# A long convolution's frequency loop on one NeuronCore: four PSUM banks written in one run of matmuls, a sum moved into the inverse transform, and row scales for two row blocks at once

## The chip, the cores and the metric

The kernel runs on one core of a Trainium2 chip. The metric is device microseconds of one execution; lower is better. Two times are compared only where they differ by more than the runs of one kernel do.

## The reference

One layer works on x of 2048 positions by 1024 channels, in float32. Two thirds of the projected channels go through a gated convolution over the whole length, done in the frequency domain, and the rest through a pooling branch:

```python
h = rms_norm(x, pre_g)
p = h @ w_in
hy = short_conv(p[..., :HYENA_IN])            # v and two gates, 512 channels each
k_f = two_sided_spectrum(hyena_filters(...))  # two filters of 2L samples for each channel
y = v
for o in range(2):
    y = gates[o] * (irfft(rfft(y, 2 * L) * k_f[:, o], 2 * L)[:, :L] + y * d)
y_h = rms_norm(y * silu(z_h), norm_h_g)
y_p = rms_norm(multiscale_pool(u_p) * silu(z_p), norm_p_g)
out = concat(y_h, y_p) @ w_out
return x + rms_norm(out, post_g)
```

## The kernel before

TensorE is written PE, VectorE DVE, ScalarE ACT, GpSimd POOL, SyncE SP. P is 128. The program has four parts, one after the other in the profile: projections, filters and pooling (to 646 us), eight frequency loops (646 to 1241), a short rest of the last gate (to 1258), and the output stage (1258 to 1404).

**The transforms.** The 512 channels are taken as four groups q of 128, and the convolutions as o = 0 and 1. Each transform has a stage of 128x128 matmuls (`s1`, `s1k`, and `gate` or `py1` on the way back), a transpose in blocks of 32 on DVE (`trans`), and a stage of 32x32 matmuls, which is the frequency loop `gloop(o, q)`. `BS[q]` holds the signal's half-done transform, `BK[o, q]` that of the filter. `gx`, `gk` and `gi` are tables of cosines and sines, laid out for 32x32 matmuls.

**The loop.** `gloop` returns a list of pieces for eight values of m. `PB` is one PSUM tile of four banks, [128, 4 banks, 4 slots, 128]: a matmul of row group i writes 32 partitions of one slot of one bank, and each piece touches all four banks. The pieces are:

- `kern(m)`: 32 matmuls transform the filter into slots 2 and 3 (L735, table `gk`), and ACT copies both slots to the SBUF tile `kk` (L742).
- `mult(m)`: 32 matmuls transform the signal into slots 0 and 1 (L735, table `gx`), DVE multiplies both slots by `kk` into `yt` (L748), and POOL adds the two halves of `yt` (L749).
- `back(m)`: 16 matmuls take the sum back into slot 2 (L756, table `gi`), and ACT copies it into `BS` (L757).

The list is `kern(0)`, `mult(0)` behind `kern(1)`, and then `back(m-1)`, `kern(m+1)`, `mult(m)` in turn, with `back(7)` at the end. The trace records each float32 matmul twice, so that 32 matmuls show as x64.

**What stands between the pieces.** `run(main, *sides)` writes the program's order by hand: the main list's pieces stand at even distances, and the pieces of the side lists are dealt among them. The sides of a loop prepare and finish other channel groups: `pre_k` and `pre_s` or `post0` (matmuls L603 to L605 in groups of six into PSUM tile `s` or `py`), and `fills`, the pooling half of the output product (L834 to L836, twelve 512-column matmuls into `fp`). The eight loops are called so, with fewer sides in the last:

```python
run(gloop(0, 0), seq(pre_k(0, 1), pre_s(1)), fills(5, 9))
...
run(gloop(1, 3, held), post1(2), [lambda ct=ct: split_wo(...) for ct in range(4)])
```

A scheduler may then move instructions a little; each engine runs its own list in order, and an instruction that waits holds back all that stand behind it on that engine.

**The output stage.** For each of 16 row blocks l2, `out_mm` writes two halves dh of 512 channels, 12 matmuls each (`mm_out`, L834 to L836), into two banks of `PB`. `finish` then has DVE scale both halves and add the pooling half `o` that a DMA brings (L965), ACT square and sum each half (L968), DVE add the two sums (L972) and make the reciprocal root `rp` in nine short operations (`rstd`, L189 to L200), DVE scale by `rp` and the gain (L979), POOL add x (L980), and SP send the rows out. `split_y`, `py1` and `stat_y` prepare the next four row blocks meanwhile.

## Time and profile before

| | |
|---|---|
| time, median of 3 runs | 1406.27 us (1402.15 to 1408.11) |
| the profiled execution's own time | 1406.32 us |
| its span in the trace | 1404.1 us |
| mean granted TensorE clock | 0.93 |
| PE busy | 1204.8 us (86% of the span) |
| DVE busy | 775.3 us (55%) |
| POOL busy | 484.6 us (35%) |
| ACT busy | 416.8 us (30%) |

The span runs from the first to the last instruction that the profiler recorded; the execution's own time is 2.2 us more. Shares of busy time are means over stages. A number in brackets behind a row of the timeline is the engine's idle time just before, with the instruction that ended it.

### The profile page before, as it was taken

Reading aid. Unit: us, or ns where it says so; the run is one execution under the profiler, and the core shown is the slowest. Engines: PE = TensorE matmul, PEld = TensorE weight load, DVE = VectorE, ACT = ScalarE, POOL = GpSimd, SP = SyncE. Lnnn points to the kernel's source line nnn. Section 1 sums busy time; section 2 is a strip of 40 time slices with the busy share of each in tenths; the row PEclk is TensorE's granted clock in tenths of the full one; section 3 lists DMA queues with packets and bytes.
Section 4 is the critical chain, followed back from the end, with each engine's and each line's share of the span. In section 5 each row is a group of like instructions: output and inputs, shape, how many; then the busy total and the mean of one; then the engine's idle time right before and its main releaser. Section 6 shows DMA issues by size and latency. Waiting matters only on the chain. (4 is left out here: it accounts for less than half of the span.)

```text
span 1404.1 us, 35240 instructions
## 1 busy us (share of the span) xinstructions
PE 1204.8 (86%) x15528; PEld 938.8 (67%) x15528; DVE 775.3 (55%) x1255; ACT 416.8 (30%) x643; POOL 484.6 (35%) x436
## 2 busy tenths in 40 slices
PE   7999999999999989979888887989788846477775
PEld 5788888788889989956556564657465534256554
DVE  6962664465467657635355645373655543137665
ACT  7521202121121121033435353343353532222211
POOL 2211104145518557532143432121343421223433
PEclk9999999999999999989999988999999976579999
DMA  7222304222333352287322324444313322053563
GB/s 247 74 79 75 95 26 124 81 97 93 132 104 95 114 147 91 75 289 237 122 89 61 105 70 133 137 120 137 96 62 110 119 78 85 2 168 129 182 210 128
DMA packets 102481, 162.15 MB, mean 115 GB/s; under 512 B 9257, under 2 KB 58169, under 8 KB 101049
## 3 DMA queue, kind: packets, MB, share of 16 engines
q1 hardware_dynamic: 100504, 156.94, 35.1%
q8 instruction: 121, 1.98, 0.6%
q10 hardware_dynamic: 1648, 2.44, 0.5%
q0 software_dynamic: 176, 0.53, 0.1%
q14 instruction: 32, 0.25, 0.1%
HBM read 113.22 MB, written 45.61 MB: 113 GB/s over the span
## 5 line engine op out<-in xcount | busy, mean ns | idle before, releaser
L749 POOL TENSOR_TENSOR yt<-yt 128x512 f32<-128x512 f32 x64 | 82.3, 1286 | 260.7 <-DVE yt L748 258.1
L557 PE MATMUL nm<-wh,XH 128*128 128x256 f32 x512 | 144.7, 283 | 8.0 <-DVE a L564 7.1
L748 DVE TENSOR_TENSOR yt<-PB,kk 128x1024 f32<-128x1024 f32 x64 | 78.0, 1219 | 121.3 <-PE PB L735 121.0
L559 PE MATMUL nm<-wh,XL 128*128 128x256 f32 x512 | 144.7, 283 | 0.0
L558 PE MATMUL nm<-wl,XH 128*128 128x256 f32 x512 | 144.7, 283 | 0.0
L564 DVE SCALAR_TENSOR_TENSOR a<-nm,r_nat,wc 128x256 f32<-128x256 f32 x192 | 81.5, 475 | 50.6 <-DMA wc<-cw 14.1
L557 PEld LDWEIGHTS nm<-wh,XH 128*128 128x128 f32 x512 | 97.7, 191 | 9.1 <-DVE a L564 8.3
L324 PE MATMUL mm<-XH,wh 128*128 128x512 f32 x256 | 103.0, 402 | 0.0
L756 PE MATMUL PB<-yt,gi 32*32 32x128 f32 x2048 | 35.3, 303 | 78.3 <-POOL yt L749 78.3
L326 PE MATMUL mm<-XH,wl 128*128 128x512 f32 x256 | 102.2, 399 | 0.0
L325 PE MATMUL mm<-XL,wh 128*128 128x512 f32 x256 | 101.5, 396 | 0.0
L559 PEld LDWEIGHTS nm<-wh,XL 128*128 128x128 f32 x512 | 96.7, 189 | 0.0
L558 PEld LDWEIGHTS nm<-wl,XH 128*128 128x128 f32 x512 | 96.6, 189 | 0.0
L735 PE MATMUL PB<-BS,gx 32*32 32x128 f32 x4096 | 77.5, 317 | 12.7 <-ACT kk L742 10.8
L630 DVE STREAM_TRANSPOSE BS<-BS 128x1024 f32<-128x1024 f32 x64 | 74.2, 1213 | 22.6 <-ACT BS L713 12.8
L735 PE MATMUL PB<-BK,gk 32*32 32x128 f32 x4096 | 75.7, 309 | 11.7 <-ACT BS L757 10.1
L756 PEld LDWEIGHTS PB<-yt,gi 32*32 32x32 f32 x2048 | 16.1, 108 | 102.1 <-POOL yt L749 101.6
L757 ACT COPY BS<-PB 128x512 f32<-128x512 f32 x64 | 39.8, 622 | 148.8 <-PE PB L756 148.8
L742 ACT COPY kk<-PB 128x1024 f32<-128x1024 f32 x64 | 64.8, 1012 | 59.5 <-PE PB L735 59.2
L735 PEld LDWEIGHTS PB<-BS,gx 32*32 32x32 f32 x4096 | 49.9, 112 | 43.9 <-ACT kk L742 18.4
L735 PEld LDWEIGHTS PB<-BK,gk 32*32 32x32 f32 x4096 | 48.8, 109 | 39.7 <-ACT BS L757 23.5
L686 POOL TENSOR_TENSOR sd<-ab 128x512 f32<-128x512 f32 x32 | 54.2, 1692 | 60.8 <-DVE ab L682 60.7
(216 smaller groups left out, 3030.8 us busy)
## 6 DMA issues: line engine op xcount, KB each, us to landing
fy<-yp_d SPq DMA_DIRECT2D x32, 512.0 KB
dec<-t_dec SPq DMA_DIRECT2D x30, 512.0 KB
wr<-w SPq DMA_DIRECT2D x16, 512.0 KB
ut<-v_d SPq DMA_DIRECT2D x32, 256.0 KB
op_d<-fo SPq DMA_DIRECT2D x32, 256.0 KB
gt<-g_d SPq DMA_DIRECT2D x32, 256.0 KB
o<-op_d SPq DMA_DIRECT2D x32, 256.0 KB
xt<-x SPq DMA_DIRECT2D x16, 512.0 KB
```

Of the source, the lines that this page charges most:

```text
L324: T.matmul(ps, wh, XH[lb][:, d], start=(d == 0), stop=False)
L325: T.matmul(ps, wh, XL[lb][:, d], start=False, stop=False)
L326: T.matmul(ps, wl, XH[lb][:, d], start=False, stop=(d == NT - 1))
L557: T.matmul(ps, xh[:, d, ls], wh, start=(d == 0), stop=False)
L558: T.matmul(ps, xh[:, d, ls], wl, start=False, stop=False)
L559: T.matmul(ps, xl[:, d, ls], wh, start=False, stop=(d == NT - 1))
L564: V.scalar_tensor_tensor(out=a[s], in0=ps, scalar=r_nat[:, l2:l2 + 1], in1=wc[:, s], op0=ALU.mult, op1=ALU.mult)
L630: V.transpose(out=ap, in_=ap)
L735: ins = T.matmul(PB[32 * i:32 * i + 32, j, slot + k], tab[js, 4 * m + i, k], B[js, 2 * m + i // 2, :, i % 2], start=True, stop=True)
L742: S.copy(out=kk, in_=PB[:, :, 2:4])
L748: V.tensor_tensor(out=yt, in0=PB[:, :, 0:2], in1=kks.pop(m), op=ALU.mult)
L749: G.tensor_tensor(out=yt[:, :, 0], in0=yt[:, :, 0], in1=yt[:, :, 1], op=ALU.add)
```

## The change

A loop step is now one function, `step(t)`, which writes all four slots in one run of up to 80 matmuls and then reads them. It is called for t = -1 to 8, so the list has 10 pieces where it had 24.

- The way back for t-1 takes both halves of the product `cd` and adds them in PSUM: 32 accumulating matmuls into slot 3, in place of the POOL addition and 16 matmuls. `gi` is twice as large.
- The signal's transform for t has 16 matmuls into slot 0, where 32 went into slots 0 and 1: the second half was the first with other signs, which the tables `gk` and `gi` now hold. `gx` is half as large.
- The filter's transform for t+1 keeps its 32 matmuls, into slots 1 and 2.
- The readers follow: DVE multiplies slot 0, broadcast over two halves, by `kk` (L753 of the kernel after); ACT copies slot 3 into `BS` (L756) and slots 1 and 2 into the next `kk` (L762).
- `PB` has a pool of its own, closed ahead of the output stage, which takes its two halves from a pool of four one-bank tiles `po`.
- `finish` is split. `scale` has one square over 1024 elements in place of two over 512; `norm` makes `rp` for two row blocks at once (twelve operations on two elements in place of ten on one, twice). The last two row blocks are done alone, and the buffers of `o` go by pairs.

```diff
     psB = pool(ph2, "psB", 1, PS)
 
-    PB = psB.tile([P, 4, 4, P], F32, name="PB")
+    pst = ExitStack()
+    psL = pool(pst, "psL", 1, PS)
+    PB = psL.tile([P, 4, 4, P], F32, name="PB")
...
     def gloop(o, q, after=None):
         u = f"{o}{q}"
-        kks, yts = {}, {}
+        kks, cds = {}, {}
         order = [(j, (j + d) % 4) for d in range(4) for j in range(4)]
-        def fwd(B, tab, m, slot):
-            for k in range(2):
-                for j, i in order:
-                    js = slice(32 * j, 32 * j + 32)
-                    ins = T.matmul(PB[32 * i:32 * i + 32, j, slot + k], tab[js, 4 * m + i, k],
-                                   B[js, 2 * m + i // 2, :, i % 2], start=True, stop=True)
-            return ins
-
-        def kern(m):
-            fwd(BK[o, q], gk, m, 2)
-            kk = wp.tile([P, 4, 2, P], F32, tag="kk", name=f"kk{u}_{m}", bufs=2)
-            S.copy(out=kk, in_=PB[:, :, 2:4])
-            kks[m] = kk
-
-        def mult(m):
-            fwd(BS[q], gx, m, 0)
-            yt = fp.tile([P, 4, 2, P], F32, tag="yt", name=f"yt{u}_{m}", bufs=3)
-            V.tensor_tensor(out=yt, in0=PB[:, :, 0:2], in1=kks.pop(m), op=ALU.mult)
-            G.tensor_tensor(out=yt[:, :, 0], in0=yt[:, :, 0], in1=yt[:, :, 1], op=ALU.add)
-            yts[m] = yt
-
-        def back(m):
-            yt = yts.pop(m)
-            for i, j in order:
-                js = slice(32 * i, 32 * i + 32)
-                ins = T.matmul(PB[32 * j:32 * j + 32, i, 2], gi[js, m, j], yt[js, j, 0], start=True, stop=True)
-            S.copy(out=BS[q][:, 2 * m:2 * m + 2].rearrange("p a c i -> p a i c"),
-                   in_=PB[:, :, 2].rearrange("p (a i) c -> p a i c", i=2))
-            if after:
-                after(m, ins)
-
-        r = [lambda: kern(0)]
-        for m in range(8):
-            if m:
-                r.append(lambda m=m: back(m - 1))
-            if m + 1 < 8:
-                r.append(lambda m=m: kern(m + 1))
-            r.append(lambda m=m: mult(m))
-        r.append(lambda: back(7))
-        return r
+        def step(t):
+            if t > 0:
+                cd = cds.pop(t - 1)
+                for k in range(2):
+                    for i, j in order:
+                        js = slice(32 * i, 32 * i + 32)
+                        ins = T.matmul(PB[32 * j:32 * j + 32, i, 3], gi[js, k, t - 1, j], cd[js, j, k],
+                                       start=(k == 0), stop=(k == 1))
+            for m, B, tab, slots in ((t, BS[q], gx, (0,)), (t + 1, BK[o, q], gk, (1, 2))):
+                if 0 <= m < 8:
+                    for k, sl in enumerate(slots):
+                        for j, i in order:
+                            js = slice(32 * j, 32 * j + 32)
+                            w = tab[js, 4 * m + i, k] if len(slots) > 1 else tab[js, 4 * m + i]
+                            T.matmul(PB[32 * i:32 * i + 32, j, sl], w, B[js, 2 * m + i // 2, :, i % 2],
+                                     start=True, stop=True)
+            if 0 <= t < 8:
+                cd = fp.tile([P, 4, 2, P], F32, tag="cd", name=f"cd{u}_{t}", bufs=3)
+                V.tensor_tensor(out=cd, in0=PB[:, :, 0:1].broadcast_to([P, 4, 2, P]), in1=kks.pop(t), op=ALU.mult)
+                cds[t] = cd
+            if t > 0:
+                S.copy(out=BS[q][:, 2 * t - 2:2 * t].rearrange("p a c i -> p a i c"),
+                       in_=PB[:, :, 3].rearrange("p (a i) c -> p a i c", i=2))
+                if after:
+                    after(t - 1, ins)
+            if t < 7:
+                kk = wp.tile([P, 4, 2, P], F32, tag="kk", name=f"kk{u}_{t + 1}", bufs=2)
+                S.copy(out=kk, in_=PB[:, :, 1:3])
+                kks[t + 1] = kk
+        return [lambda t=t: step(t) for t in range(-1, 9)]
...
+    pst.close()
+    psO = pool(pst, "psO", 1, PS)
...
-                ps = PB[:, 2 * (i % 2) + dh].rearrange("p s c -> p (s c)")
+                ps = psO.tile([P, 512], F32, tag="po", name=f"po{l2}_{dh}", bufs=4)
...
-    def finish(lb, rr, i, pss):
+    hs = (slice(0, 512), slice(512, 1024))
+    live = {}
+    def scale(lb, rr, i, pss):
         l2 = 4 * lb + i
         xt = wp.tile([P, D], F32, tag="kk", name=f"xt{l2}", bufs=2)
         Q.dma_start(out=xt, in_=xv[:, l2])
-        if l2 % 5 > 2:
-            o_ = abp.tile([P, D], F32, tag="ab", name=f"o{l2}", bufs=2)
-        else:
-            o_ = wp.tile([P, D], F32, tag=("sd", "dd")[l2 % 2], name=f"o{l2}", bufs=2)
+        tg = ("sd", "dd", "ab")[l2 // 2 % 3]
+        o_ = (abp if tg == "ab" else wp).tile([P, D], F32, tag=tg, name=f"o{l2}", bufs=2)
         for dh in range(2):
             Q.dma_start(out=o_[:, dh * 512:dh * 512 + 512], in_=op_d[dh, l2])
-        hs = (slice(0, 512), slice(512, 1024))
+        if l2 % 2 == 0 or l2 == 15:
+            live["ss"] = op.tile([P, 2], F32, tag="ss2", name=f"ss{l2}", bufs=2)
+        ss = live["ss"][:, l2 % 2:l2 % 2 + 1]
         s2 = op.tile([P, 2], F32, tag="s2", name=f"s2{l2}", bufs=2)
         for dh, ds in enumerate(hs):
             V.scalar_tensor_tensor(out=o_[:, ds], in0=pss[dh], scalar=rr[:, i:i + 1], in1=o_[:, ds],
                                    op0=ALU.mult, op1=ALU.add)
-            sq = fp.tile([P, 512], F32, tag="sq", name=f"sq{l2}_{dh}", bufs=2)
-            S.activation(out=sq, in_=o_[:, ds], func=AF.Square, accum_out=s2[:, dh:dh + 1])
             if l2 == 15:
+                sq = fp.tile([P, 512], F32, tag="sq", name=f"sq{l2}_{dh}", bufs=1)
+                S.activation(out=sq, in_=o_[:, ds], func=AF.Square, accum_out=s2[:, dh:dh + 1])
                 G.tensor_tensor(out=o_[:, ds], in0=o_[:, ds], in1=pg[:, ds], op=ALU.mult)
-        ssum = op.tile([P, 1], F32, tag="ssum", name=f"ssum{l2}", bufs=2)
-        V.tensor_tensor(out=ssum, in0=s2[:, 0:1], in1=s2[:, 1:2], op=ALU.add)
-        rp = op.tile([P, 1], F32, tag="rp", name=f"rp{l2}", bufs=2)
-        rstd(op, rp, ssum, D, 1, "rp1")
-        for ds in hs if l2 > 13 else (slice(0, 1024),):
-            if l2 == 15:
-                V.scalar_tensor_tensor(out=o_[:, ds], in0=o_[:, ds], scalar=rp, in1=xt[:, ds], op0=ALU.mult, op1=ALU.add)
-            else:
-                V.scalar_tensor_tensor(out=o_[:, ds], in0=o_[:, ds], scalar=rp, in1=pg[:, ds], op0=ALU.mult, op1=ALU.mult)
-                G.tensor_tensor(out=o_[:, ds], in0=o_[:, ds], in1=xt[:, ds], op=ALU.add)
-            Q.dma_start(out=ov[:, l2, ds], in_=o_[:, ds])
+        if l2 == 15:
+            V.tensor_tensor(out=ss, in0=s2[:, 0:1], in1=s2[:, 1:2], op=ALU.add)
+        else:
+            sq = fp.tile([P, D], F32, tag="sq", name=f"sq{l2}", bufs=1)
+            S.activation(out=sq, in_=o_, func=AF.Square, accum_out=ss)
+        live[l2] = xt, o_
+    def norm(l2s):
+        n = len(l2s)
+        c0 = l2s[0] % 2
+        rp = op.tile([P, 2], F32, tag="rp", name=f"rp{l2s[0]}", bufs=2)[:, 0:n]
+        rstd(op, rp, live["ss"][:, c0:c0 + n], D, n, f"rp{n}")
+        for k, l2 in enumerate(l2s):
+            xt, o_ = live.pop(l2)
+            for ds in hs if l2 > 13 else (slice(0, 1024),):
+                if l2 == 15:
+                    V.scalar_tensor_tensor(out=o_[:, ds], in0=o_[:, ds], scalar=rp[:, k:k + 1], in1=xt[:, ds],
+                                           op0=ALU.mult, op1=ALU.add)
+                else:
+                    V.scalar_tensor_tensor(out=o_[:, ds], in0=o_[:, ds], scalar=rp[:, k:k + 1], in1=pg[:, ds],
+                                           op0=ALU.mult, op1=ALU.mult)
+                    G.tensor_tensor(out=o_[:, ds], in0=o_[:, ds], in1=xt[:, ds], op=ALU.add)
+                Q.dma_start(out=ov[:, l2, ds], in_=o_[:, ds])
...
-            finish(lb, rr, i, pss)
+            scale(lb, rr, i, pss)
+            l2 = 4 * lb + i
+            if l2 > 13:
+                norm([l2])
+            elif i % 2:
+                norm([l2 - 1, l2])
+    pst.close()
```

In the first loop's list of PE, before, the three pieces of a step stand with other matmuls between them; `fp` and `s` are side products.

```order
L835 MATMUL fp_6186<-fl_5322,fy_6184 128x512
L756 MATMUL PB<-yt_2_6009,gi 32x128 [waits Pool_49]
L756 MATMUL PB<-yt_2_6009,gi 32x128 x15
L836 MATMUL fp_6186<-fh_5321,fy_6184 128x512
...
L735 MATMUL PB<-BK_5299,gk 32x128 [waits Activation_49]
L735 MATMUL PB<-BK_5299,gk 32x128 x31
L834 MATMUL fp_6186<-fh_5321,fy_6184 128x512
...
L735 MATMUL PB<-BS_5288,gx 32x128 [waits Activation_49]
L735 MATMUL PB<-BS_5288,gx 32x128 x31
```

The same place after the change, up to the next step:

```order
L829 MATMUL fp_6203<-fh_5324,fy_6201 128x512
L741 MATMUL PB<-cd_3_6078,gi 32x128 [waits DVE_49,Activation_49]
L741 MATMUL PB<-cd_3_6078,gi 32x128 x31
L749 MATMUL PB<-BS_5291,gx 32x128 x16
L749 MATMUL PB<-BK_5302,gk 32x128 x32
L830 MATMUL fp_6203<-fl_5325,fy_6201 128x512
L831 MATMUL fp_6203<-fh_5324,fy_6201 128x512
L603 MATMUL s_01_3_6221<-ut_3_6219,f1s 128x256 [waits DMAHW3_49,PE_49]
...
L831 MATMUL fp_6442<-fh_5324,fy_6440 128x512
L741 MATMUL PB<-cd_4_6176,gi 32x128 [waits DVE_49,Activation_49]
```

Three blocks with a wait each have become one block with one wait, and the side matmuls stand together between two blocks: here five of 512 columns and eighteen of 256.

On ACT, at the same place before, the two copies of a step stand apart, and each waits for PE:

```order
L757 COPY BS_5288<-PB 128x2x2x128 [waits DVE_49,PE_49]
L742 COPY kk_4_6064<-PB 128x1024 [waits PE_49,Activation_49]
L857 ACTIVATE fo_6199<-fp_6186,rpn 128x512 [waits DMAHW1_49,PE_49]
L713 COPY BS_6102<-s_01_3_6204 128x2x2x128 [waits PE_49]
```

After the change:

```order
L756 COPY BS_5291<-PB 128x2x2x128 [waits DVE_49]
L762 COPY kk_4_6081<-PB 128x1024 [waits Activation_49]
L852 ACTIVATE fo_6216<-fp_6203,rpn 128x512 [waits DMAHW1_49,PE_49]
L715 COPY BS_6085<-s_01_3_6221 128x2x2x128 [waits PE_49]
L756 COPY BS_5291<-PB 128x2x2x128 [waits DVE_49]
```

The two copies stand side by side; the first waits for DVE, whose product reads the same banks, and the second for the first.

On DVE in the output stage before, the first of the two L965 waits for PE, and the chain of one row block follows:

```order
L965 SCALAR_TENSOR_TENSOR o_14597<-PB,rr_14450,o_14597 128x512 [waits DMAHW1_49,DMAHW3_49,PE_49,Pool_49]
L965 SCALAR_TENSOR_TENSOR o_14597<-PB,rr_14450,o_14597 128x512 [waits DMAHW4_49]
L972 TENSOR_TENSOR ssum_14607<-s_14600 128x1 [waits Activation_49]
L189 TENSOR_SCALAR rp1v<-ssum_14607 128x1 [waits DVE_49]
```

After the change:

```order
L966 SCALAR_TENSOR_TENSOR o_14156<-po_0_14128,rr_14113,o_14156 128x512 [waits DMAHW1_49,DVE_49,DMAHW5_49,PE_49,Pool_49]
L966 SCALAR_TENSOR_TENSOR o_14156<-po_1_14141,rr_14113,o_14156 128x512 [waits DMAHW2_49,PE_49]
L966 SCALAR_TENSOR_TENSOR o_14193<-po_0_14165,rr_14113,o_14193 128x512 [waits DMAHW3_49,DMAHW6_49,PE_49,Pool_49]
L966 SCALAR_TENSOR_TENSOR o_14193<-po_1_14178,rr_14113,o_14193 128x512 [waits DMAHW4_49,PE_49]
L189 TENSOR_SCALAR rp2v<-ss_14159 128x2 [waits Activation_49]
```

Each half now has its own wait for PE and its own bank, and the short operations stand behind four halves.

## Rows read from the trace of the kernel before

**Rows 1.** Busy time by stretch: start:end, us, engines' busy us, granted clock, DMA share, GB/s.

```profile
725.69:798.18 72.49, 61.26 (x1463) 41.53 (x1464) 41.89 (x51) 32.73 (x53) 28.32 (x21) 0.93 0.26 80
798.18:881.01 82.83, 66.50 (x1461) 44.44 (x1461) 44.70 (x54) 35.30 (x57) 27.34 (x21) 0.85 0.29 91
646.15:1087.74 441.59, 376.69 (x8815) 254.90 (x8816) 235.32 (x272) 180.77 (x281) 141.13 (x106) 0.93 0.35 108
1164.15:1241.00 76.85, 38.35 (x1282) 26.44 (x1283) 19.00 (x19) 18.52 (x24) 16.15 (x12) 0.59 0.18 57
1258.00:1404.10 146.10, 107.07 (x451) 82.82 (x449) 95.10 (x270) 33.72 (x81) 54.74 (x28) 0.93 0.51 165
```

**Rows 2.** The page's costliest groups: busy us, mean ns, idle before with releaser.

```profile
L749 POOL TENSOR_TENSOR yt<-yt 128x512 f32<-128x512 f32 x64 | 82.3, 1286 | 260.7 <-DVE yt L748 258.1
...
L756 PE MATMUL PB<-yt,gi 32*32 32x128 f32 x2048 | 35.3, 303 | 78.3 <-POOL yt L749 78.3
...
L735 PE MATMUL PB<-BS,gx 32*32 32x128 f32 x4096 | 77.5, 317 | 12.7 <-ACT kk L742 10.8
...
L735 PE MATMUL PB<-BK,gk 32*32 32x128 f32 x4096 | 75.7, 309 | 11.7 <-ACT BS L757 10.1
```

**Rows 3.** Timeline of one step in the last loop, with no side work (PEld left out).

```profile
1201.26 1.23 DVE L748 TENSOR_TENSOR yt<-PB,kk 128x1024 f32<-128x1024 f32 x1 [7.26 <-PE PB L735]
1202.57 1.26 POOL L749 TENSOR_TENSOR yt<-yt 128x512 f32<-128x512 f32 x1 [7.23 <-DVE yt L748]
...
1203.88 0.74 PE L756 MATMUL PB<-yt,gi 32*32 32x128 f32 x32 [2.76 <-POOL yt L749]
1204.79 0.61 ACT L757 COPY BS<-PB 128x512 f32<-128x512 f32 x1 [5.25 <-PE PB L756]
...
1205.45 1.53 PE L735 MATMUL PB<-BK,gk 32*32 32x128 f32 x64 [0.83 <-ACT BS L757]
1207.02 1.01 ACT L742 COPY kk<-PB 128x1024 f32<-128x1024 f32 x1 [1.62 <-PE PB L735]
...
1208.08 1.52 PE L735 MATMUL PB<-BS,gx 32*32 32x128 f32 x64 [1.10 <-ACT kk L742]
1209.75 1.23 DVE L748 TENSOR_TENSOR yt<-PB,kk 128x1024 f32<-128x1024 f32 x1 [7.26 <-PE PB L735]
```

**Rows 4.** Timeline of PE around one 32x32 block among 128x128 matmuls, second loop.

```profile
739.43 0.28 PE L605 MATMUL py<-dd,f1s 128*128 128x256 f32 x1
739.65 1.09 PE L735 MATMUL PB<-BK,gk 32*32 32x128 f32 x64
740.67 0.38 PE L603 MATMUL s<-ut,f1s 128*128 128x256 f32 x1
740.90 0.28 PE L604 MATMUL s<-ut,f1s 128*128 128x256 f32 x1
741.01 0.28 PE L605 MATMUL s<-ut,f1s 128*128 128x256 f32 x1
```

**Rows 5.** Timeline of one DVE product behind another DVE instruction, last loop.

```profile
1178.35 1.09 PE L735 MATMUL PB<-BS,gx 32*32 32x128 f32 x64
...
1181.14 0.69 DVE L925 TENSOR_TENSOR yb<-yc,yb 128x512 fp32r<-128x512 f32 x1 [4.86 <-ACT yb L924]
...
1181.75 1.22 DVE L748 TENSOR_TENSOR yt<-PB,kk 128x1024 f32<-128x1024 f32 x1
```

**Rows 6.** Timeline of one row block in the output stage, PE and DVE.

```profile
1328.16 1.41 DVE L965 SCALAR_TENSOR_TENSOR o<-PB,rr,o 128x512 f32<-128x512 f32 x2 [1.71 <-PE PB L836]
...
1329.63 0.50 PE L834 MATMUL PB<-O,yb 128*128 128x512 f32 x1 [1.56 <-DVE o L965]
...
1332.54 1.29 DVE L979 SCALAR_TENSOR_TENSOR o<-o,rp,pg 128x1024 f32<-128x1024 f32 x1
...
1335.54 1.41 DVE L965 SCALAR_TENSOR_TENSOR o<-PB,rr,o 128x512 f32<-128x512 f32 x2 [1.72 <-PE PB L836]
```

**Rows 7.** PE's groups from 1258 us on: busy us, mean ns, idle before with releaser.

```profile
L834 PE MATMUL PB<-O,yb 128*128 128x512 f32 x64 | 29.2, 456 | 23.8 <-DVE o L965 23.7
```

More of the change, by code (lines that the diff above doesn't have):

```diff
@@ L52, in _tables @@
     g = np.arange(32)
-    gx = np.zeros((128, 32, 2, 32))
+    gx = np.zeros((128, 32, 32))
     gk = np.zeros((128, 32, 2, 32))
-    gi = np.zeros((4, 32, 8, 4, 32))
+    gi = np.zeros((4, 32, 2, 8, 4, 32))
     n2 = np.arange(16)
@@ L67, in _tables @@
         q = slice(j * 32, j * 32 + 32)
-        gx[q, :, 0] = np.concatenate([re, im], axis=2)
-        gx[q, :, 1] = np.concatenate([-im, re], axis=2)
+        gx[q] = np.concatenate([re, im], axis=2)
         pr = np.concatenate([rows, 16 + rows])
-        gk[q, :, 0] = np.concatenate([re, re], axis=2)[pr]
-        gk[q, :, 1] = np.concatenate([im, im], axis=2)[pr]
+        gk[q, :, 0] = np.concatenate([re, im], axis=2)[pr]
+        gk[q, :, 1] = np.concatenate([im, re], axis=2)[pr]
         psi = phi + (np.pi * (kk + 0.25) / 128)[:, None, None]
         c, s = np.cos(psi).transpose(0, 2, 1), np.sin(psi).transpose(0, 2, 1)
-        b = np.concatenate([np.concatenate([c, s], axis=2), np.concatenate([-s, c], axis=2)], axis=1)
-        gi[:, :, :, j] = b.reshape(8, 4, 32, 32).transpose(1, 2, 0, 3)
-    gi = gi.reshape(128, 8, 4, 32)
+        re, im = np.concatenate([c, s], axis=2), np.concatenate([-s, c], axis=2)
+        for k, b in enumerate((np.concatenate([re, -re], axis=1), np.concatenate([im, im], axis=1))):
+            gi[:, :, k, :, j] = b.reshape(8, 4, 32, 32).transpose(1, 2, 0, 3)
+    gi = gi.reshape(128, 2, 8, 4, 32)
     t = np.linspace(0.0, 1.0, L, dtype=f32)
@@ L617, in build @@
     fp = pool(ph2, "fp")
-    gx = fp.tile([P, 32, 2, 32], F32, tag="gx", name="gx")
+    gx = fp.tile([P, 32, 32], F32, tag="gx", name="gx")
     gk = fp.tile([P, 32, 2, 32], F32, tag="gk", name="gk")
-    gi = fp.tile([P, 8, 4, 32], F32, tag="gi", name="gi")
+    gi = fp.tile([P, 2, 8, 4, 32], F32, tag="gi", name="gi")
     fwp = pool(ph2, "fwp")
     psB = pool(ph2, "psB", 1, PS)
-    PB = psB.tile([P, 4, 4, P], F32, name="PB")
+    pst = ExitStack()
+    psL = pool(pst, "psL", 1, PS)
+    PB = psL.tile([P, 4, 4, P], F32, name="PB")
     fst = ExitStack()
@@ L901, in build @@
     yb3 = kp.tile([P, 2, 4, 512], F32R, tag="BS", name="yb3", bufs=2)
-    pg = fp.tile([P, D], F32, tag="gi", name="pg")
+    pg = fp.tile([P, D], F32, tag="gx", name="pg")
     Q.dma_start(out=pg, in_=I["pg"].broadcast_to([P, D]))
-    O1 = [fp.tile([P, 4, 512], F32R, tag=t_, name=f"O1{t_}") for t_ in ("gx", "gk")]
+    O1 = [fp.tile([P, 4, 512], F32R, tag=t_, name=f"O1{t_}") for t_ in ("gi", "gk")]
     for ct in range(4):
```

## The prediction

> **What bounds the kernel now.** I read the stretches first. In loops 1 to 6 PE is busy 376.7 of 441.6 us and DVE 235 [rows 1]: PE is the engine that is nearly full, so its idle time and its busy time both count there. In loop 8, which has few side products, PE is busy only 38.4 of 76.9 us at a granted clock of 0.59, near the lower level of 1.2 GHz. The output stage keeps PE busy 107.1 of 146.1 us.
>
> The costliest groups then tell where PE idles in the loops: 78.3 us ahead of the way back, waiting for POOL's sum, 12.7 ahead of the signal's and 11.7 ahead of the filter's transform [rows 2]. Together that is 102.7 us, the pool from which the loop part of the change can draw.
>
> The timeline of a bare step in loop 8 shows how such a wait is made [rows 3]. DVE multiplies (start 1201.26), POOL adds (1202.57), PE transforms back (1203.88), ACT copies (1204.79), PE does the filter (1205.45), ACT copies (1207.02), PE does the signal (1208.08), DVE multiplies again at 1209.75. All is in one row: the step takes 8.49 us, in which PE works 0.74 + 1.53 + 1.52 = 3.79 and idles 2.76 + 0.83 + 1.10 = 4.69. In loops 1 to 7 side matmuls stand in these holes and cover most of them.
>
> **The bare step after.** PE still has 80 matmuls (32 back, 16 signal, 32 filter, for 16, 32 and 32), so I keep 3.79 us; 32 accumulating matmuls are taken at the 1.52 of 32 plain ones. Then the readers come in turn, as the new order says: ACT's first copy waits for DVE, the second for the first, and the next block for both. From [rows 3]: 0.15 from the last matmul to DVE (1208.08 + 1.52 to 1209.75), 1.31 from DVE's start to the instruction that waits for it, 0.61 for the first copy, 1.06 from the second copy's start to PE. That makes 3.13 us idle, and a step of 6.92: 1.57 less. POOL's addition, one of PE's three returns and two semaphore handoffs are gone; three reads of PSUM in a row are what is late next. The product reads slot 0 twice instead of two slots; no row has such a read. Below, its writing of 1024 elements is unchanged, so I allow no gain on 1.23; above, a second pass over the operand would cost 1.23 more. I take 1.23, the row with the same output.
>
> The Trainium skill (PSUM — Partial Sum Buffer, "PSUM bank collisions raise a hardware error") says that two engines may not touch the same partitions of one bank at the same time, two readers included. No run here shows two readers at once; if ACT could copy beside DVE, PE's hole would be about 1.9 us and loop 8 would gain some 10 us more.
>
> *Loop 8.* Its 8 steps are nearly bare: 8 x 4.69 = 37.5 of its 38.5 us of PE idle time [rows 1, 3]. **Gain 8 x 1.57 = 12.5 us.** The clock stays as it is in the likeliest case, since PE still pauses in every step.
>
> *Loops 1 to 7, waits.* Of 102.7 us, 65 remain for these 56 steps, 1.16 us each. After the change a step has one hole of 3.13, and all side work lies in it. In the new order I priced what stands between two blocks by PE's starting intervals (0.12 for 256 columns [rows 4]; 0.24 for 512, a row block's PE time of [rows 6] over its 24 matmuls, worked out below). The place shown in the order above holds 5 x 0.24 + 18 x 0.12 = 3.4 us, enough. 43 of the 56 gaps hold 2.9 us or more; the others, most of them at the end of a loop where 0.95 to 2.4 us stand, lack 17 us, and the first steps, whose signal part still waits for a copy, 3 more: 20 us left. To that I add a price for queueing. The product can stand behind other work on DVE: [rows 5] show the last matmul end at 1179.44 (1178.35 + 1.09), an instruction that waited for ACT hold DVE until 1181.83, and the product start at 1181.75, 2.2 us later than at the bare 0.15. Between nothing [rows 3] and this I take 0.15 us on the mean of 56 steps, 8 us, since I took the row for its length and many gaps have cover to spare. Queued behind a late product are ACT's two copies and then the next block on PE, so a delay goes straight to PE where the cover is just 3.1. **Gain 65 - 28 = 37 us.**
>
> *Switches.* A 32x32 block among 128x128 matmuls costs PE time at both ends: from the last 256-column matmul to the block 0.22 us (739.43 to 739.65), and 0.23 from the first behind it to the second, where 0.11 is usual (740.90 to 741.01) [rows 4]. That is 0.1 + 0.1 a block. The order has 166 such blocks before and 75 after. Of the 91 fewer some 20 stand in loop 8 or behind a wait that hides the switch: 70 x 0.2. **Gain 14 us**, bounds 0 and 18.
>
> *Output stage.* A row block begins on PE at 1329.63 only because both L965, 1.41 us together, must have read two regions of one tile [rows 6]: 1.56 us of PE idle time for each, and 23.7 us over the stage [rows 7]. After, PE waits only for the bank of four halves ago. From one first L965 to the next, 1328.16 to 1335.54, a row block takes 7.38 us; without that wait it takes what PE needs, 7.38 - 1.56 = 5.8. DVE must then serve two blocks in 11.6 us: four halves at 0.71, two L979 at 1.29, and the short operations, 3.0 us with the wait for ACT's squares (1329.57 to 1332.54) for ten and so at most 3.6 for twelve, are 9.0 us together, plus the preparation of y. DMA moves 165 GB/s over 146.1 us at a share of 0.51; in 125 us it would be 193 at 0.60 [rows 1]. Nothing there is full. The last two blocks are done alone as before, so the tail after the last matmul stays. **Gain 21 us** of 23.7, since the wait for the row scale `rr` of a new group of four stays.
>
> **Sum**, against the profiled execution's 1406.3 us, which is the median of the runs to 0.1: 1406.3 - 12.5 - 37 - 14 - 21 = 1322.
>
> POOL's 82.3 us of additions [rows 2] fall away too; POOL is on no path but the one priced. Larger and smaller tables have the same bytes together and are loaded in the first part, behind other work. One square over 1024 elements stands on ACT, busy 33.7 of 146.1 us there [rows 1], and delays `norm` by half a microsecond a pair, under DVE's slack.
>
> **Rivals.**
> 1. *The output stage gets another bound* (0.20). Scaling by pairs makes DVE's short operations and two L979 come in a lump of 6 us, and the next halves queue behind them; with four banks PE can run ahead 5.8 us at most. Half of the gain or all of it goes: 1332 to 1343. Against it: DVE's sum of 9.0 in 11.6.
> 2. *The denser PE gets more clock* (0.15). Loop 8 is at 0.59 [rows 1]; a step with PE busy 3.79 of 6.92 in one piece instead of 3.79 of 8.49 in three could be granted 2.4 GHz, in which case up to 1.9 us a step fall away, 15 us, and the holes' queueing need not come, 8 more: about 1297.
> 3. *The longer hole costs clock* (0.10). Loop 3 did the work of loop 2 (1461 matmuls against 1463) at 0.85 instead of 0.93, and PE was busy 66.5 instead of 61.3 us: 5.2 us. Where a hole of up to 3 us in each step of loops 1 to 6 does this to all, 6 x 5.2 = 31: 1353. Against it: the three holes before, of 4.69 together, left loops 1 to 6 at 0.93. [...]
> 4. *The side work was the bound* (0.06). If in loops 1 to 7 the sides' own chains over DVE, ACT and DMA set the pace (DVE is busy 41.9 of loop 2's 72.5 us [rows 1]), the holes move to the sides' matmuls and only loop 8 and the output stage gain: 1406.3 - 33.5 = 1373.
> 5. *Slower* (0.04). A step's readers are now one chain on two engines with no other order. If the product waits 2.2 us behind side work [rows 5] in each of 56 steps, that is 123 us instead of 8: 1437. It decides from 1.65 us a step on: the loop's waits and switches, the output stage and loop 8 give 92 us before queueing, over 56.
>
> **The numbers.** The likeliest case, 0.45, is 1322, within 1308 and 1332 for the bounds of switches and queueing. Rival 2 lies below, 1, 3 and 4 above, all faster than before. About 0.5% (7 us) is what a measurement of this kernel tells from no change. Rival 5 and a product that costs a second pass on top of a lost output gain hold what is not faster: 0.94 faster, 0.02 same, 0.04 slower. A range of 1290 to 1350 leaves out part of rival 3, and rivals 4 and 5.
>
> **What would show it.** In the profile after: no POOL addition in the loops; PE idle ahead of the way back (L741) 28 us in loops 1 to 7 and about 3.1 a step in loop 8, which then takes some 64 us; the product starting 0.15 us behind the block in most steps; the first copy on ACT starting at the product's end and never beside it; about 5.8 us a row block in the output stage and no idle time of 1.5 ahead of each L834; a granted clock of 0.93 in loops 1 to 6. Wrong would make it: a clock near 0.85 there (rival 3) or near full in loop 8 (rival 2); PE idle in front of `s`, `py` or `fp` matmuls (rival 4); idle ahead of L741 of 2 us in covered steps (rival 5); PE waiting for DVE's L966 behind `norm` (rival 1).

## The result, and the profile of the kernel after

| | before | after |
|---|---|---|
| time, median | 1406.13 us (4 runs, 1402.15 to 1408.11) | 1308.12 us (4 runs, 1302.60 to 1312.22) |
| ratio, 95% interval | 1 | 0.9304 (0.9261 to 0.9346) |
| span of the profiled execution | 1404.1 us | 1308.1 us |
| mean granted clock | 0.93 | 0.948 |

The change takes 98 us off; the prediction said 84, and 1290 to 1350 for the time. The stretches tell where it went. The first fence has the loops of the kernel before, from the first block of loop 1 to the first copy of loop 8 (loops 1 to 7), and from there to the end of the last way back (loop 8); the output stage of before is in [rows 1]. Each stretch is read from one execution; four executions of the kernel after lie 10 us apart, so a few us between the stretches of two kernels prove nothing. Columns are those of [rows 1].

```profile
645.03:1164.15 519.12, 427.85 (x10297) 288.97 (x10296) 274.85 (x316) 214.85 (x333) 167.25 (x125) 0.92 0.34 106
1164.15:1240.13 75.98, 37.48 (x1281) 25.68 (x1281) 18.95 (x18) 17.90 (x23) 16.15 (x12) 0.59 0.17 53
```

The kernel after, cut at the same places: loops 1 to 7, loop 8, the rest of the gate, the output stage.

```profile
647.89:1116.88 468.99, 397.29 (x10297) 302.06 (x10296) 279.45 (x316) 203.62 (x334) 96.13 (x69) 0.93 0.38 117
1116.88:1170.33 53.45, 34.35 (x1281) 27.95 (x1281) 18.32 (x18) 17.06 (x24) 6.17 (x4) 0.69 0.22 69
1170.33:1188.37 18.04, 17.24 (x80) 14.24 (x81) 5.54 (x6) 3.99 (x6) 0.00 (x0) 0.88 0.68 226
1188.37:1308.10 119.73, 99.50 (x451) 79.99 (x449) 89.35 (x213) 30.68 (x51) 59.06 (x28) 0.94 0.58 200
```

Loops 1 to 7 gain 50.1 us, loop 8 22.5, the output stage 26.4; the part ahead of the loops is 2.9 us longer in this execution. Read the two fences once more for PE alone. In loops 1 to 7 PE's busy time falls by 30.6 us (427.9 to 397.3) and its idle time, the stretch less the busy time, by 19.6 (91.3 to 71.7): the larger part is not a wait. In loop 8 it is the other way round: 19.4 of idle time and 3.1 of busy time.

A bare step of loop 8 after the change, to be laid beside [rows 3] (PEld and pieces of the same block left out):

```profile
1148.51 1.22 DVE L753 TENSOR_TENSOR cd<-PB,kk 128x1024 f32<-128x1024 f32 x1 [5.94 <-PE PB L749]
1149.77 0.61 ACT L756 COPY BS<-PB 128x512 f32<-128x512 f32 x1 [5.66 <-DVE cd L753]
1150.27 1.01 ACT L762 COPY kk<-PB 128x1024 f32<-128x1024 f32 x1
1151.33 1.32 PE L741 MATMUL PB<-cd,gi 32*32 32x128 f32 x52 [3.04 <-ACT kk L762]
...
1153.77 1.49 PE L749 MATMUL PB<-BK,gk 32*32 32x128 f32 x61 [0.25 <-issue]
1155.36 1.23 DVE L753 TENSOR_TENSOR cd<-PB,kk 128x1024 f32<-128x1024 f32 x1 [5.62 <-PE PB L749]
```

From product to product it takes 6.85 us where 6.92 was forecast, with one hole of 3.04 us. The three readers come in turn, as the order said: the first copy 1.26 behind the product's start, the second 0.50 behind the first. There is a second hole that was not in the sum, 0.25 us inside the block, which the trace puts down to "issue": it shows nothing that PE waited for.

What PE waited for in all eight loops (us in total, times, longest); the first rows of before are in [rows 2]:

```profile
PE PB L741 <- ACT kk L762: 25.5, 16, 3.2
PE PB L741 <- ACT BS L756: 20.3, 7, 4.0
PE PB L749 <- issue: 19.8, 15, 2.8
...
PE PB L749 <- ACT kk L762: 4.4, 4, 3.4
```

102.7 us ahead of the step's matmuls have become 71.5 (the four rows above and 1.5 us more). The 19.8 us of issue are new: before, the trace has 0.3 us of it there. The seven waits for the first copy (L756) are all the last step of a loop, t = 8, which has the way back alone and no second copy ahead of it. Two of them show it: 64 records of L741, and no L749 in the block.

```profile
1109.96 1.53 PE L741 MATMUL PB<-cd,gi 32*32 32x128 f32 x64 [4.00 <-ACT BS L756]
...
1168.80 1.52 PE L741 MATMUL PB<-cd,gi 32*32 32x128 f32 x64 [2.03 <-ACT BS L756]
```

In the output stage, PE's groups after, for [rows 7]:

```profile
L829 PE MATMUL po<-O,yb 128*128 128x512 f32 x64 | 26.6, 415 | 2.6 <-DVE o L966 2.6
```

23.7 us of PE's wait have become 2.6. In sum, PE's busy time in the stage fell by 7.6 us (107.1 to 99.5), its idle time up to the last matmul by 24.4 (29.1 to 4.8), and the time from the end of the last matmul to the end of the span grew by 5.6 (9.9 to 15.5).

### The profile page after: what moved, and what is told of

Its sections match the earlier page's. It is cut to its first block, busy times and chain, and to the rows that moved or that the text cites. A ratio compares the mean times of both kernels' runs of the same rounds, so it can differ in the third digit from the quotient of the medians.

```text
span 1308.1 us, 35031 instructions
## 1 busy us (share of the span) xinstructions
PE 1165.7 (89%) x15528; PEld 953.7 (73%) x15528; DVE 773.8 (59%) x1198; ACT 401.6 (31%) x613; POOL 407.3 (31%) x372
## 5 line engine op out<-in xcount | busy, mean ns | idle before, releaser
L753 DVE TENSOR_TENSOR cd<-PB,kk 128x1024 f32<-128x1024 f32 x64 | 77.6, 1213 | 102.8 <-PE PB L749 102.8
L741 PE MATMUL PB<-cd,gi 32*32 32x128 f32 x4096 | 74.7, 305 | 46.0 <-ACT kk L762 25.5
L749 PE MATMUL PB<-BK,gk 32*32 32x128 f32 x4096 | 90.2, 309 | 19.5 <-issue 18.0
L741 PEld LDWEIGHTS PB<-cd,gi 32*32 32x32 f32 x4096 | 48.4, 109 | 71.8 <-ACT kk L762 35.1
L688 POOL TENSOR_TENSOR sd<-ab 128x512 f32<-128x512 f32 x32 | 50.7, 1585 | 137.6 <-DVE ab L684 137.6
L749 PEld LDWEIGHTS PB<-BK,gk 32*32 32x32 f32 x4096 | 64.0, 110 | 30.4 <-issue 24.5
L777 POOL TENSOR_TENSOR dd<-BS,dd 128x512 fp32r<-128x512 f32 x32 | 46.1, 1447 | 87.0 <-ACT dd L776 72.1
L762 ACT COPY kk<-PB 128x1024 f32<-128x1024 f32 x64 | 65.2, 1019 | 21.8 <-PE PB L749 13.4
L715 ACT COPY BS<-s 128x512 f32<-128x512 f32 x64 | 40.8, 640 | 94.4 <-PE s L605 94.1
L756 ACT COPY BS<-PB 128x512 f32<-128x512 f32 x64 | 39.8, 622 | 96.5 <-DVE cd L753 85.7
L696 PE MATMUL s1k<-sd,f 128*128 128x512 f32 x128 | 65.6, 630 | 2.0 <-ACT fo L852 1.0
```

Of the source, the lines that this page charges most:

```text
L696: T.matmul(ps.rearrange("p a i c -> p (a i c)"), f1[:, ri], sd[:, ri], start=True, stop=True)
L741: ins = T.matmul(PB[32 * j:32 * j + 32, i, 3], gi[js, k, t - 1, j], cd[js, j, k], start=(k == 0), stop=(k == 1))
L749: T.matmul(PB[32 * i:32 * i + 32, j, sl], w, B[js, 2 * m + i // 2, :, i % 2], start=True, stop=True)
L753: V.tensor_tensor(out=cd, in0=PB[:, :, 0:1].broadcast_to([P, 4, 2, P]), in1=kks.pop(t), op=ALU.mult)
```

## The experiments

Each was run in turn with the kernel before on one chip; ratios are to that, and the kernel after stands at 0.9304 (0.9261 to 0.9346). It was not run beside them, so ratios are the safer comparison with it. A stretch "loops 1 to 7" is cut as above, and is again one execution's.

**The two halves apart.** `loops_only` has the loops of after and the output stage of before, `out_only` the reverse.

```diff
-                ps = psO.tile([P, 512], F32, tag="po", name=f"po{l2}_{dh}", bufs=4)
+                ps = PB[:, 2 * (i % 2) + dh].rearrange("p s c -> p (s c)")
...
-            scale(lb, rr, i, pss)
+            finish(lb, rr, i, pss)
```

> The loops of the kernel after with the output stage of the kernel before. If the two halves of the change are independent, the eight loops take the 522 us that they take in the kernel after (595 before), and the output stage the 146 us that it takes before: 1308 + 26 = 1334 us. If the loops' gain needs the new output stage, or the output stage lost something to the loops, the sum misses by more than 5 us.

> The loops of the kernel before with the output stage of the kernel after. Independent halves: loops 595 us, output stage 120 us, 1406 - 26 = 1380 us, and PE's idle time ahead of L829 there 2 to 3 us instead of 23.7. If the new output stage is fast only behind the new loops, over 1390.

`loops_only` 1333.8 us, 0.9494 (0.9457 to 0.9530), its loops 521.6 us and its output stage 144. `out_only` 1372.3 us, 0.9770 (0.9732 to 0.9809), its loops 586 and its output stage 119.3. The two take 69.6 and 31.1 us off the kernel before, 101 together, where the whole change takes 98: as far as the spread of runs tells, the halves are independent. `out_only` is 8 us under what was expected. In its profile the loops took 9 us less than in that of before, although nothing in `gloop` was edited; loop 3 had a clock of 0.96 there and 0.85 in [rows 1]. Its four runs are all under 1377, so something else than one execution's clock may have a part in it; that stays open.

**One block, or no POOL addition?** `three_blocks` keeps the new mathematics and puts the three pieces of a step apart again, each with its own readers.

```diff
-        return [lambda t=t: step(t) for t in range(-1, 9)]
+        r = [lambda: kern(0)]
+        for m in range(8):
+            if m:
+                r.append(lambda m=m: back(m - 1))
+            if m + 1 < 8:
+                r.append(lambda m=m: kern(m + 1))
+            r.append(lambda m=m: mult(m))
+        r.append(lambda: back(7))
+        return r
```

> The kernel after with its mathematics (16 matmuls for the signal, 32 accumulating ones on the way back, no POOL addition), but each step in the three pieces of the kernel before: way back, filter and signal stand apart among side matmuls, each read on its own. Theory A (POOL's addition was the wait, and blocks cost only their switches): a bare step idles 1.5 + 0.83 + 1.10 = 3.4 us, takes 7.2, and loops 1 to 7 lose only the 14 us of switches: 1310 to 1325. Theory B (one block with one wait is what pays): the three waits stay in part, PE idles 30 us or more ahead of the three pieces in loops 1 to 7, over 1340.

1322.3 us, 0.9409 (0.9377 to 0.9441), as theory A had it. Its stretches, loops 1 to 7 and loop 8, and then a bare step:

```profile
650.10:1121.10 471.00, 419.10 (x10297) 285.66 (x10296) 270.62 (x316) 215.15 (x334) 97.50 (x69) 0.93 0.38 117
1121.10:1185.40 64.30, 37.27 (x1281) 25.49 (x1281) 18.43 (x18) 17.79 (x23) 6.17 (x4) 0.63 0.19 61
...
1156.98 1.52 PE L738 MATMUL PB<-cd,gi 32*32 32x128 f32 x64 [1.52 <-DVE cd L762]
1159.20 1.52 PE L750 MATMUL PB<-BK,gk 32*32 32x128 f32 x64 [0.70 <-ACT BS L740]
1161.83 0.74 PE L750 MATMUL PB<-BS,gx 32*32 32x128 f32 x32 [1.10 <-ACT kk L756]
1164.09 1.52 PE L738 MATMUL PB<-cd,gi 32*32 32x128 f32 x64 [1.51 <-DVE cd L762]
```

The bare step takes 7.11 us, with holes of 1.51, 0.70 and 1.10: of the 1.64 us between 8.49 before and 6.85 after, 1.38 come without the single block. Theory A holds for the step and for the time. Theory B's sign holds too, though its time does not: PE waits 32 us ahead of the three pieces in loops 1 to 7, and the kernel is fast all the same.

Loops 1 to 7 take 471.0 us, as good as the 469.0 of after, but made up otherwise: PE is busy 21.8 us more for the same matmuls at the same mean clock, and idle 19.8 us less (51.9 against 71.7). So most of the loops' gain comes with the new mathematics, in which POOL's addition is gone: 48 us in loops 1 to 7 and 12 in loop 8 against the profile of before (42 and 9 against the loops of `out_only`). The single block takes 21.8 us of PE's busy time off in loops 1 to 7 and gives 19.8 back as idle time; only in loop 8 does it pay, 10.9 us.

**POOL back in the chain.** `pool_back` lets POOL double half of the product, which the table halves again, ahead of the way back.

```diff
+                G.tensor_tensor(out=cd[:, :, 0], in0=cd[:, :, 0], in1=cd[:, :, 0], op=ALU.add)
                 cds[t] = cd
...
-            gi[:, :, k, :, j] = b.reshape(8, 4, 32, 32).transpose(1, 2, 0, 3)
+            gi[:, :, k, :, j] = (0.5, 1.0)[k] * b.reshape(8, 4, 32, 32).transpose(1, 2, 0, 3)
```

> The kernel after with an addition on POOL put back into each step's chain: it doubles one half of the product, which the table then halves, so that the way back waits for POOL again. Theory A (POOL's 1.26 us was the wait): each bare step is 1.3 us longer, the loops lose 10 us in loop 8 and more where the cover is just 3.1 us: 1325 to 1350. Theory C (with all readers in a row, POOL works beside ACT's two copies, 1.56 us, which PE waits for anyway): a bare step stays at 6.85, within 5 us of 1308.

1331.1 us, 0.9483 (0.9445 to 0.9522): the time of theory A, but not by its mechanism. A bare step, and the block of the step after it:

```profile
1179.17 0.62 ACT L757 COPY BS<-PB 128x512 f32<-128x512 f32 x1 [7.36 <-DVE cd L753]
1179.21 1.04 POOL L754 TENSOR_TENSOR cd<-cd 128x512 f32<-128x512 f32 x1 [7.84 <-DVE cd L753]
1179.67 1.02 ACT L763 COPY kk<-PB 128x1024 f32<-128x1024 f32 x1
1180.83 1.31 PE L741 MATMUL PB<-cd,gi 32*32 32x128 f32 x52 [3.06 <-ACT kk L763]
...
1189.17 1.23 PE L741 MATMUL PB<-cd,gi 32*32 32x128 f32 x44 [5.08 <-POOL cd L754]
```

In the first, POOL works beside ACT's copies and the hole stays 3.06 us, as theory C had it. What PE waited for in the loops:

```profile
PE PB L749 <- issue: 30.7, 19, 2.8
PE PB L741 <- POOL cd L754: 24.5, 10, 5.1
PE PB L741 <- ACT kk L763: 23.0, 12, 3.6
...
PE PB L741 <- ACT BS L757: 5.7, 2, 3.0
```

In ten steps POOL came last, with waits of 2.4 us in the mean and up to 5.1. That is not all new: six of the ten are the last step of a loop, where the kernel after waits too (for the first copy, 20.3 us against 5.7 here). One step shows POOL's queue plainly: at 1185.33 its list held a 2.35 us operation for the output stage, the addition started at 1187.63, and PE waited 5.08 us. So in one block POOL's duration is hidden, and its queue was not in that step. But the loops lose 24.3 us in all, and the queue is the smaller part: PE's waits for the copies and POOL ahead of the step's matmuls grew by 6.2 us together, its busy time by 5.9, and the stalls put down to issue there by 10.9. Why these grew is open, and with it the larger part of what the addition costs.

**What "issue" is.** In after, 15 waits ahead of L749 (and three ahead of side matmuls) end with nothing that the profile shows. I counted PE's records (matmuls, weight loads, and the semaphore and drain instructions of its sequencer, in order of time, from 0): every one of the 18 stalls of the loops stands at a count of 193 or 194 modulo 256. `code_shift` puts 32 small matmuls ahead of the loops, 128 records.

```diff
+    for _ in range(32):
+        T.matmul(PB[0:32, 0, 3], f1[0:32, 0, 0:32], f1[0:32, 1], start=True, stop=True)
     run(gloop(0, 0), seq(pre_k(0, 1), pre_s(1)), fills(5, 9))
```

> The kernel after with 32 small matmuls more (128 PE instructions in the trace) ahead of the first loop, into a slot that is overwritten later. Theory D (code arrives 256 PE instructions at a time): the stalls put down to issue stay at the same counts modulo 256 of PE's instructions, and so move to other matmuls of the blocks; their sum stays between 10 and 30 us. Theory E (a stall belongs to a place in the block, such as the change from one table to the next): they stay ahead of the same matmuls, at counts 128 higher. The time by both is 1303 to 1318 us.

1316.5 us, 0.9381 (0.9357 to 0.9404), 19.9 us of stalls in the step's blocks. The counts of the first stalls, from the two traces:

```
after       7873  8641  9410  11201  11970  13761   modulo 256: 193 193 194 193 194 193
code_shift  8385  9153  9410  10946  11714  13506   modulo 256: 193 193 194 194 194 194
```

The stalls stay on the grid of 256 and stand ahead of other matmuls of the program: theory D, not E. In the loops of all fourteen traces 196 of the 199 waits put down to issue stand at 193 or 194; the other three are those of `split_readers` below. The profile's row for the queue that loads code, after, gives the unit (packets, MB, share of the engines): 2.00 MB / 122 = 16 KB a packet. PE's 31206 records make 121.9 units of 256, so the 122 packets are about PE's code and no other's.

```profile
q8 instruction: 122, 2.00, 0.6%
```

One stall is shown in full by PE's timeline. Between 1145 and 1147.6 the trace has one packet of this queue, which started at 1145.4 and took 0.96 us; PE goes on 1.2 us after its end. So it is at every one of the 196: PE goes on 1.1 to 1.6 us after the end of a packet of this queue.

```profile
1145.93 1.08 PE L749 MATMUL PB<-BK,gk 32*32 32x128 f32 x34
1147.56 0.73 PE L749 MATMUL PB<-BK,gk 32*32 32x128 f32 x28 [0.54 <-issue]
```

A block of 80 matmuls has 320 records, more than one such unit, and PE runs through it faster than the next unit comes: one block with no stall took 2.35 us (1124.37 to 1126.72), and two packets never start less than 3.4 us apart in these loops. In `three_blocks`, with the same number of records but no block over 128, the step's matmuls have no such stall. The Trainium skill (Runtime: NRT & Kernel Launch, "Instruction fetch mechanics") says that an engine's code comes in blocks of 16 KiB, 256 instructions, loaded ahead while the block before runs. The runs agree with the size; they differ where the Trainium skill calls this loading hidden, by 20 us here.

**Two blocks.** `two_blocks` has the way back and the signal in one (`both`, 192 records) and the filter in another (`kern`, 128).

```diff
-        return [lambda t=t: step(t) for t in range(-1, 9)]
+        r = [lambda: kern(0)]
+        for m in range(9):
+            r.append(lambda m=m: both(m))
+            if m < 7:
+                r.append(lambda m=m: kern(m + 1))
+        return r
```

> The kernel after with the step in two blocks: way back and signal (192 instructions in the trace), read by DVE and ACT, and then the filter (128), read by ACT, with side matmuls between. Theory D: no block holds 256 instructions, so the stalls put down to issue fall under 5 us (19.8 in after), while the switches of some 60 blocks more cost 10 to 15 us: 1300 to 1315. If only the number of waits counted, the second wait in each step would cost 0.4 us or more bare and the time would rise over 1320.

1313.6 us, 0.9357 (0.9338 to 0.9376). The stalls fall to 4.2 us (5 times), as expected, and PE is busy 408.6 us in loops 1 to 7, between one block and three. What is saved goes into the second wait: PE waits 34.7 us for the first copy ahead of the filter. Loops 1 to 7 take 467.2 us, loop 8 60.4. One, two and three blocks stand within 4 us of each other in loops 1 to 7. For PE's busy time the three kernels give one price: the traces show 72, 119 and 164 blocks of 32x32 matmuls in these loops, and 11.3 us more for 47 blocks or 21.8 for 92 are both 0.24 us a block.

**Side work later.** `sides_later` deals the sides over 94% of a loop's list.

```diff
-    def run(main, *sides, upto=0.88):
+    def run(main, *sides, upto=0.94):
```

> The kernel after with the side work of each loop dealt over 94% of the list instead of 88%. The prediction put 17 us of uncovered holes at the ends of the loops: by that the last gaps are covered better and the time falls by 3 to 8 us. If the delays of the readers behind other work on DVE and ACT make the holes, wherever the side matmuls stand, no change within 3 us; if the next loop then waits for its inputs, slower by up to 10.

1298.1 us (1290.9 to 1307.4), 0.9243 (0.9210 to 0.9275), 10 us under after; the intervals overlap a little. Loops 1 to 7 take 457.2 us, 11.8 less: 6.6 of idle time, and 5.2 of busy time at a clock of 0.95 for 0.93. The waits for the first copy, which are the loops' last steps, come to 9.4 us against 20.3, 7 times each. So there were holes at the ends, as the prediction's pricing of the gaps said.

**The reads cut by banks.** `split_readers` lets DVE read banks 0 and 1 while ACT reads 2 and 3, and then the reverse.

```diff
+            for h in range(2):
+                if 0 <= t < 8:
+                    b = slice(2 * h, 2 * h + 2)
+                    V.tensor_tensor(out=cds[t][:, b], in0=PB[:, b, 0:1].broadcast_to([P, 2, 2, P]), in1=kk0[:, b],
+                                    op=ALU.mult)
+                c = 1 - h
+                b = slice(2 * c, 2 * c + 2)
+                if t > 0:
+                    S.copy(out=BS[q][:, 2 * t - 2 + c].rearrange("p c i -> p i c"), in_=PB[:, b, 3])
+                if t < 7:
+                    S.copy(out=kks[t + 1][:, b], in_=PB[:, b, 1:3])
```

> The kernel after with the three reads of a step cut by banks: DVE takes banks 0 and 1 while ACT copies banks 2 and 3, and then the other way round, so that PE's hole should fall from 2.9 us to about 1.9. Theory A (the readers' chain bounds the bare step): a bare step falls from 6.85 to about 5.8, loop 8 by 5 to 8 us and the whole to 1295 to 1303. Theory D (the stalls that the trace of after puts down to issue, 18 us ahead of L749, come from PE's code, which arrives 256 instructions at a time: a block has 320 instructions): PE reaches the next 256 sooner and waits there instead, the stalls grow over 20 us, and the time stays within 5 us of 1308.

1312.7 us, 0.9346 (0.9326 to 0.9367): no gain. The idea was not tested, because ACT still waited for DVE's half, though it reads other banks. PE also stood still three times for 3.4 us ahead of side matmuls, which the trace puts down to issue and which is not explained:

```profile
1149.37 0.69 DVE L759 TENSOR_TENSOR cd<-PB,kk 128x512 f32<-128x512 f32 x1 [4.97 <-PE PB L749]
1150.09 0.39 ACT L764 COPY BS<-PB 128x256 f32<-128x256 f32 x1 [4.80 <-DVE cd L759]
...
1152.62 1.33 PE L741 MATMUL PB<-cd,gi 32*32 32x128 f32 x52 [3.35 <-ACT kk L766]
```

`split_tiles` makes the four banks two tiles of two.

```diff
-    PB = psL.tile([P, 4, 4, P], F32, name="PB")
+    PB = [psL.tile([P, 2, 4, P], F32, name=f"PB{h}") for h in range(2)]
```

> The reads cut by banks once more, now with the four banks as two tiles of two banks, because in split_readers ACT still waited for DVE's half. If the two engines now read at the same time, a bare hole is 0.15 + two halves of about 0.7 and the handoffs, 1.7 to 2.0 us instead of 3.0, and a bare step 5.6 to 5.9. Theory A (the readers' chain is the bound): 1295 to 1303. Theory D (PE's code is the bound of a dense step: 320 instructions a step, and 256 in no less than about 4.9 us from one load to the next, as after shows): a step cannot fall under about 6.1 us, stalls put down to issue rise over 25 us, and the time is 1300 to 1310.

1293.5 us (1286.9 to 1295.9), 0.9219 (0.9191 to 0.9247): clear of after's interval, and the fastest but one. A step of loop 8:

```profile
1133.43 0.69 DVE L759 TENSOR_TENSOR cd<-PB,kk 128x512 f32<-128x512 f32 x1 [4.62 <-PE PB L749]
1133.43 0.39 ACT L764 COPY BS<-PB 128x256 f32<-128x256 f32 x1 [4.58 <-PE PB L749]
...
1135.11 1.33 PE L741 MATMUL PB<-cd,gi 32*32 32x128 f32 x52 [1.75 <-ACT kk L766]
...
1138.64 0.69 DVE L759 TENSOR_TENSOR cd<-PB,kk 128x512 f32<-128x512 f32 x1 [3.62 <-PE PB L749]
```

The two engines start at the same time, the hole is 1.75 us, and this step, which has no stall, takes 5.21. Theory A holds for the step. Theory D's floor of 6.1 us a step falls: I had taken its 4.9 us for a unit of code from one place, where packets of code start as little as 3.4 us apart, and the stalls' sum is 20.2 us, no more than in after. The gain stands in loops 1 to 7 (447.3 us against 469.0, of which 17.3 are idle time); the profiled execution is the fastest of six, 6.6 us under their median, so this is the upper end. Loop 8 takes 53.1, as in after: one step there takes 11 us from product to product, because an instruction ahead of the copies in ACT's list waits for a DMA.

`split_later` adds 94% to that.

> split_tiles with the side work dealt over 94% of each loop's list, as in sides_later. If the two edits act on different holes (the readers' chain, and the uncovered ends of the loops), their gains add: 10 us less than split_tiles, 1285 to 1298. If the shorter hole is covered anyway in all gaps with side work, it gives what sides_later gave, 1298.

1291.3 us (1287.0 to 1299.1), 0.9208 (0.9177 to 0.9239): not to be told from `split_tiles`, and 7 us under `sides_later`, with overlapping intervals. The two edits do not add: in loops 1 to 7 PE's waits ahead of the step's matmuls fall from 41.8 to 26.5 us, and those ahead of side matmuls rise from 12.3 to 27.5. This is 17 us under the kernel after.

**The output stage's two parts.** `banks_only` has the four one-bank tiles with the old `finish`, `pairs_only` the pairs with the regions of `PB`.

Each is one of the two edits of `loops_only` by itself: `banks_only` the second, `pairs_only` the first.

> The kernel after with the output banks from a pool of four tiles, but the old way of finishing: a square for each half and a reciprocal root for each row block. If PE's wait for the two halves was the bound, as the prediction had it, the output stage takes the 120 us of after: 1308. If DVE's short operations were a bound of their own, it takes 125 us or more: over 1313.

> The kernel after with row scales for two blocks at once, but the output in four regions of the one tile PB, as before. By the prediction's step PE waits about 1.5 us ahead of each row block again, 23 us in all, and the stage takes 144 to 147 us: 1331 to 1335. If the short operations were the bound, it keeps a good part of the gain: under 1325.

`banks_only` 1320.1 us, 0.9414 (0.9383 to 0.9446); `pairs_only` 1341.9 us, 0.9561 (0.9523 to 0.9599). Their output stages:

```profile
1192.30:1322.40 130.10, 101.99 (x450) 81.93 (x449) 108.23 (x270) 34.74 (x81) 55.21 (x28) 0.90 0.56 184
1187.00:1337.60 150.60, 108.44 (x450) 83.56 (x449) 87.20 (x213) 30.52 (x51) 60.96 (x28) 0.91 0.46 160
```

Against 146.1 us before, the banks alone give 16, the pairs alone cost 4.5, and both together give 26.4. With the banks free, DVE is busy 108.2 of 130.1 us and PE waits for it again (8.6 us ahead of L829); with pairs as well, DVE is busy 89.4 of 119.7. DVE's short operations are not only many but stretched: L196, on one element, takes 228 ns in the mean in the stage before and 331 in `banks_only`. At the end of after an operation of L200 on one element took 2.21 us (from 1291.78), beside an addition on POOL, where the same line takes 0.16 us elsewhere; that POOL is the reason was not tested.

## Why the prediction was right, and where its terms were wrong

The time came out in the range, 14 us under the forecast, with each of the four terms off by 5 us or more.

*Loops 1 to 7.* Waits and switches were to give 37 + 14 = 51 us, and the stretch gave 50.1. That is chance. Ahead of the step's matmuls PE's waits in these loops fell from 64.3 us to 50.0, by 14 and not by 37. The readers' part of the sum came out. Three rows make up most of the 50.0:

```profile
PE PB L749 <- issue: 19.0, 13, 2.8
PE PB L741 <- ACT BS L756: 18.3, 6, 4.0
PE PB L741 <- ACT kk L762: 10.3, 10, 2.0
```

28.6 us stand ahead of L741, where 28 were left in: 18.3 at the last step of six loops, where the sum put 17 at the ends, and 10.3 in ten other steps. The step that failed is a term put at nothing without a reason: PE's own code, 19.0 us in 13 stalls. The sum left 28 us of waits for a denser PE and did not ask whether anything but readers could stop it.

Switches were sized too small, 14 for 21.8 us of PE's busy time between three blocks and one. The price was nearly right, 0.24 us a block for 0.2. The count was low: 20 of the 91 fewer blocks were set aside for loop 8 or behind a wait, but in the traces 89 of the 91 stand in loops 1 to 7. The other 8.8 us of busy time came with a clock that was 0.85 in loop 3 before [rows 1] and 0.94 after; `out_only` shows that the same loops can differ by 6.6 us of busy time between two executions.

*Loop 8.* 22.5 us for 12.5. The bare step was right (6.85 for 6.92). "Its 8 steps are nearly bare" was wrong on both sides. From the first product to the last, seven steps took 65.4 us before; three of them took 10.4 to 11.0, since the product stood behind a DVE instruction of the output stage (L925), as in [rows 5]. After, they took 46.7: the loop's few side matmuls, in five gaps before, now stand in three larger ones and cover the hole there; the step from 1135.99 to 1141.35, for one, took 5.36 us. PE's busy time fell by 3.1 us more with a granted clock of 0.69 for 0.59. Rival 2 was right in that, and only there: loops 1 to 7 stand at 0.93 for 0.92. (Its own sum should read 1299, 1322 less 15 and 8.)

*Output stage.* 26.4 us for 21. "PE waits only for the bank of four halves ago" was the larger part, 16 us alone. Two steps failed. "The tail after the last matmul stays" did not hold: it grew by 5.6 us. And "Nothing there is full" failed once the banks were free: without the pairs DVE is busy for 83% of the stage and holds PE up. Pairs were priced at nothing and are worth 10 us, but only where the banks are free.

*The rivals.* Rival 1's lump of DVE work did not bind: PE waited 2.6 us for L966. Rival 3's lower clock did not come. Rival 4 would have left the loops' idle time where it was. Rival 5's delay behind side work is seen in single steps: the ten waits of 10.3 us above are 1.0 us in the mean, in place of 56 of 2.2.

What the change is worth by its parts, from the experiments: the new mathematics without POOL's addition 60 us (before to `three_blocks`, loops alone; 51 against the loops of `out_only`), a step in one block 13 (`three_blocks` to after, 11 of it in loop 8), the output stage 26.

## What to carry to other kernels

A wait that side work covers is worth what the cover leaves open, and merging pieces moves the cover too: price the gaps in the new order, the last step of a loop above all, and not the bare step alone. Count the instructions of a dense run on PE: runs of 320 records stalled 15 times in the loops of after, runs of 192 and 128 in turn five times, and runs of up to 128 at most twice in a kernel (not at all in `three_blocks`, 0.3 us before, 1.8 us in `out_only`). In the long runs the engine outran its own program, and the trace calls that idle time "issue". A buffer cut into separate tiles can free an engine by more than a shorter operation does: four one-bank tiles gave 16 us, and two tiles for the loop's readers some 12 to 15 more.
